# A hybrid decoder layer: early gathered rows issued behind the fortieth scatter column, and eight of the gathered tile instead of sixteen

## The chip, the core and the metric

The kernel runs on one core of one Trainium2 chip. Its engines work side by side, each through its own list of instructions: TensorE (PE in the profile; PEld are its weight loads), VectorE (DVE), ScalarE (ACT), GpSimd (POOL) and SyncE (SP, which here only issues DMAs). GpSimd issues the indirect DMAs, by which rows are gathered from DRAM or single numbers scattered into it. The metric is the device time of one execution in microseconds (us), as the median of several.

## The reference, cut to what matters

One layer for 528 positions of width 1024: two branches (a diagonal state space model and a matrix memory) are merged, and then comes the part that the change touches, a retrieval from 16384 experts. For each of the 512 output positions and each of 8 heads it scores 2 x 128 keys, takes the 16 best pairs, and adds up the chosen experts' output rows.

```python
def block(xb):
    q = (xb @ w_q).astype(f32).reshape(PEER_TOKEN_BLOCK, PEER_HEADS, 2, PEER_HALF)
    s = jnp.einsum('thid,hikd->thik', q, keys32)
    sv, si = lax.top_k(s, PEER_TOPK)
    ...
    cs, ci = lax.top_k(cand, PEER_TOPK)
    eidx = jnp.take_along_axis(cidx, ci, axis=-1)
    gate = jax.nn.softmax(cs, axis=-1)
    ug = u_tab[eidx]
    act = jax.nn.gelu(jnp.einsum('td,thkd->thk', xb, ug).astype(f32))
    vg = v_tab[eidx]
    return jnp.einsum('thk,thkd->td', (gate * act).astype(vg.dtype), vg)
```

Each chosen expert has a row of 1024 numbers in `u_tab` (dotted with the position's vector to give an activation) and one in `v_tab` (added to the output with the weight gate times activation).

## The kernel before, in words

The 512 positions are four tiles of 128. Tiles 1, 2 and 3 (but for the last 32 positions of tile 3) go the dense way. For every one of the 128 first keys j, `hidden` (line 1090) multiplies 128 experts' u rows with the 352 positions, all of them: 8 blocks of 3 matmuls, since each number is split into a high part `uh` (ACT, line 82) and a low part `ul` (DVE, line 83). Which experts were really chosen is then put in by gate tables. `gates` (line 1441) builds them for 32 positions at a time: DVE compares indices and weights them (tiles `o12` and `ow`, both tt at line 1049), PE multiplies the two into PSUM (tile `gp`, line 1496), ACT copies that to `stg`, and SP writes `stg` to DRAM. One block of 32 positions, of tile 1, comes otherwise: `scatter` (line 1412) has POOL add its gates into DRAM, one column of 128 numbers with one indirect DMA (tile `gds`, line 1416). There are 96 columns, 12 to a head, and the first column of a head waits until those of the head before it have landed.

Tile 0 and the last 32 positions of tile 3 go the sparse way: their rows are gathered. A gather is one indirect DMA on POOL that brings 128 rows of 1024 numbers (512 KB) into a tile; its use on DVE is one product with accumulation over those 1024 numbers. For the 32 positions of tile 3 there are 32 gathers of u rows (line 1360, index tile `xsi`, used at line 1368). For tile 0 there are 128 of u rows and 128 of v rows (line 1139, index tile `e0`, used at lines 1146 and 1154).

Three stages matter here.

- While the gate tables are built, the 32 gathers of tile 3 and the first NEARLY = 16 of tile 0 are done early (`ge0` to `ge47`). They have NE = 6 buffers: `ge6` takes the buffer of `ge0` and so on.
- In the main loop (line 1633), over the 128 second-stage keys j, PE multiplies the weighted gates with v rows (tile `o`, 18 matmuls an iteration) and, in 44 iterations, does a `hidden` that was not done before. The other 256 - NEARLY gathers of tile 0 (`g16` to `g255`) are spread evenly over it, with 7 buffers of their own.
- `gi` is the load of the gate tables for 8 values of j in the loop, from what `gates` and `scatter` wrote.

The order in the first stage is planned while the program is built. `clock` counts the time of PE's work so far (0.48 us for a block of `hidden`, 0.46 per pass for a gate group), `done` counts DVE's, and `fill` (line 1523) hands out `hidden` work so that PE's share keeps step with DVE's. `fill` calls `beside` (line 1380), which plans POOL's list with a time `t` of its own: a column advances it by 2.2 (5.0 at a head's first), a gather by 1.65 (3.0 if no columns are left), and it stops when it is ahead of `clock`. Each gather is due LAG = 24 after that time; when `clock` has reached this, its use is placed behind DVE's latest instructions (`pinned`, line 1373). POOL keeps the order of its list. At run time nothing waits for `clock`: an instruction runs when its data and its buffer are there and those ahead of it on its engine are done.

The lines of `beside` that decide between a gather and a column, before:

```python
if e["got"] < e["may"] and e["got"] - e["used"] < NE and (e["turn"] or not cols):
    n, e["turn"] = e["got"], 0
    ...
elif cols:
    scatter(1)
    e["turn"] = e["columns"] % 4
```

So after a column whose number is not a multiple of 4 a gather may follow. `may` is 0 until the indices `xsi` stand in the program, 32 from there, and 32 + NEARLY once `e0` does.

Of the kernel before, what the change touches and what calls it, by code (L numbers as in the profile page):

```python
# [66 lines left out]
def tile_hybrid_block(ctx: ExitStack, tc: tile.TileContext, a: dict, out: bass.AP, dbg: dict | None = None):  # L67
# [59 lines left out]

    xh, xl, blanks = front(tc, a, dbg, cst, dram, xnp, ident, h2d, xsd, gds, x0, qt01, dump, split, mm3, rsqrt, rsqrt_cols)
    peer(tc, a, out, dbg, cst, dram, xh, xl, blanks, ident, h2d, xsd, gds, x0, qt01, dump, split, mm3, rsqrt_cols)


# [894 lines left out]
def peer(tc, a, out, dbg, cst, dram, xh, xl, blanks, ident, h2d, xsd, gds, x0, qt01, dump, split, mm3, rsqrt_cols):  # L1026
# [10 lines left out]
    NREST = NKEY // 2 - LEFT // 2  # L1037
    SPP = [k + LEFT // 2 for k in range(NREST) if k * NSP // NREST != (k - 1) * NSP // NREST]
    SP_ = [2 * k + n for k in SPP for n in range(2)]
    NEARLY = 16  # L1040
    NSIDE = MS * P // P
    LAST = 3

# [8 lines left out]
    with es:  # L1052
# [129 lines left out]
        for n in (0, 1):  # L1182
            r = 0
            x = [sum(CNT[:r]) if n == 0 else CNT[r - 1] if r else 0 for r in range(TOPK)]
            while r < (8, TOPK)[n]:
                e = r + 1
# [144 lines left out]
        cols = []  # L1331


        NE = 6
        LAG = 24.0
        early = dict(t=8.0, columns=0, due=[], got=0, used=0, may=0, turn=0, last=None)

        def spread():

# [15 lines left out]
        def fetch_early(n, t):  # L1355

            if n >= NSIDE:
                return fetch(n - NSIDE, t)
            rows["s", n] = t
            return GP.indirect_dma_start(out=t, out_offset=None, in_=a["u"],  # L1360
                                         in_offset=bass.IndirectOffsetOnAxis(ap=xsi[:, n:n + 1], axis=0))

        def use_early(n):

            if n >= NSIDE:
                return pinned(use(n - NSIDE))
            g = rows.pop(("s", n))
            pinned(V.scalar_tensor_tensor(g, g, 1.0, xrep, op0=OP.mult, op1=OP.mult,
                                          accum_out=hsi[:, n:n + 1]))
            if n == NSIDE - 1:  # L1370
                sided()
# [8 lines left out]
        def beside(flush=False):  # L1380


            e = early
            while True:
                t = 1e9 if flush else clock[0]
                while e["due"] and e["due"][0] <= t:
                    e["due"].pop(0)
                    use_early(e["used"])
                    done[0] += 1.3
                    e["used"] += 1  # L1390
                if e["t"] > t:
                    break
                e["t"] = max(e["t"], clock[0] - 8.0)
                if e["got"] < e["may"] and e["got"] - e["used"] < NE and (e["turn"] or not cols):
                    n, e["turn"] = e["got"], 0
                    k = n % NE
                    if k < 4:
                        r = up.tile([P, D], F32, tag="vraw", name=f"ge{n}", bufs=4)
                    else:
                        r = rw.tile([P, D], F32, tag=f"early{k}", name=f"ge{n}", bufs=1)  # L1400
                    e["last"] = tc.keep_in_program_order(fetch_early(n, r))
                    e["t"] += 1.65 if cols else 3.0
                    e["due"].append(e["t"] + LAG)
                    e["got"] += 1
                elif cols:
                    scatter(1)
                    e["turn"] = e["columns"] % 4
                    e["t"] += 2.2 if e["columns"] % CH_ else 5.0
                elif e["got"] == e["may"] or not flush:
                    break  # L1410

        def scatter(n):

            early["columns"] += len(cols[:n])
            for ix, wt, c in cols[:n]:
                i_ = GP.indirect_dma_start(out=gds.rearrange("i g b j t -> (i g b j t)").unsqueeze(1),  # L1416
                                           out_offset=bass.IndirectOffsetOnAxis(ap=ix[:, c:c + 1], axis=0),
                                           in_=wt[:, c:c + 1], in_offset=None, compute_op=OP.add)

                h = c // CH_  # L1420
                if c % CH_ == 0:
                    heads.append([])
                for o in heads[h]:
                    tc.declare_no_dep(i_.ins, o.ins, reason="columns of one head")
                for o in heads[h - 1] if h else blanks:
                    behind(i_, o)
                heads[h].append(i_)
                behind(i_, lows[-1])
                if early["last"]:
                    tc.add_manual_dep(i_.ins, early["last"].ins.name, mybir.DependencyInfo(  # L1430
                        mybir.DependencyClass.NoSync, mybir.DependencyReason.DATA), reason="order")
            del cols[:n]
# [87 lines left out]

        whole = 4 * 24 + 40 * 2.5 + (NSIDE + NEARLY) * 1.3 + 3

        def fill(us):

            done[0] += us
            if paced[0]:
                beside()
            while todo and (ntodo - len(todo)) * whole < done[0] * ntodo:
                j, h = todo.pop(0)
                hidden(j, 2 * h, 2 * h + 2)  # L1530
# [26 lines left out]
        def more():  # L1557
            yield from filled(2)
            yield from filled(0)
            placed(prs[0][1].rearrange("p h k -> p (h k)"), 0)  # L1560
            V.tensor_copy(e0, prs[0][1].rearrange("p h k -> p (h k)"))
            early["may"] = NSIDE + NEARLY
        rest = more()
# [5 lines left out]
        assert early["used"] >= NSIDE, early  # L1569
        gates(3, rest, [P // TB - 1])  # L1570
        beside(True)
        for j, h in todo:
            hidden(j, 2 * h, 2 * h + 2)
# [14 lines left out]
        def products(i, j, wh, wl, vh, vl, pin=None, halves=(0, 1)):  # L1588
            s_ = slice(i * P, (i + 1) * P)
            for c in halves:  # L1590
                cc = slice(c * 512, (c + 1) * 512)
                last = mm3(op_[i][:, cc], wh[:, s_], wl[:, s_], vh[:, cc], vl[:, cc], j == 0, j == NKEY - 1, pin)
            return last
# [37 lines left out]
        due = 0  # L1631
        loop[0] = True
        for j in range(NKEY):
# [21 lines left out]

            upto = min(j + 1, NKEY - 6) * (2 * P - NEARLY) // (NKEY - 6)
            for last in (0, 1):
                while due < (upto if last else min(due + 1, upto)):
                    n = NEARLY + due
                    due += 1  # L1660
# [18 lines left out]
            if j < NKEY - LAST:  # L1679
                for i in range(NTD):  # L1680
                    last = products(i, *ops[j])
# [93 lines left out]
```

## Time and profile before

| | us |
|---|---|
| median of 3 runs | 1694.6 (1692.6 to 1696.47) |
| profiled execution, its own time | 1700.12 |
| its span, first to last instruction | 1698.2 |
| early rows: from the first early gather's issue (661.7) to the last early use (about 946) | 284.3 |
| main loop, from about 976 to about 1676 | 700 |

In rows of the profile, a name such as `ge<-ge,qt` says what an instruction writes and reads, `xN` how many instructions a row groups, and a bracket at the end of a row, as in `[3.53 <-DMA ge<-in_u,xsi]`, how long the engine was idle before it and what ended that. PEclk is TensorE's granted clock as a share of full speed. Matmuls follow each other before the one ahead is through, so PE's busy time is no measure of its work; its idle time is.

### The profile page before, as it was taken

What the parts mean: (1) busy time and instruction counts of PE and PEld (TensorE: products, weight loads), DVE (VectorE), ACT (ScalarE), POOL (GpSimd) and SP (SyncE); (2) the same over time, 40 slices, a digit from 0 to 9 for tenths busy, and PEclk for the clock granted to TensorE, in tenths of its full rate; (3) what the DMA queues carried; (4) which work ended last, traced back from release to release, by engine and by line L of the source; (5) the groups of instructions that cost most, each with busy time, mean ns of one, the idle gap of its engine ahead of it and who ended that gap; (6) DMA issues with size and microseconds to landing.
All of it is one profiled execution on the core that took longest, in us unless ns stands there. A gap on an engine that the chain in (4) does not pass through costs nothing. (4 is left out here: it accounts for less than half of the span.)

```text
span 1698.2 us, 25640 instructions
## 1 busy us (share of the span) xinstructions
PE 1631.2 (96%) x9551; PEld 1441.0 (85%) x9551; DVE 1318.4 (78%) x2639; ACT 710.3 (42%) x1159; POOL 685.7 (40%) x474
## 2 busy tenths in 40 slices
PE   7999999999999999979988899999999999999997
PEld 7898787878888899979988888888888888888885
DVE  6996733366579899979876497887979879797986
ACT  4544554433333254546544533333433334333334
POOL 2000032222132663677777243343434556554630
PEclk9999999999999999989989999999999999999998
DMA  4514252214453266889988999998989999999973
GB/s 177 126 51 112 96 186 92 63 38 135 165 186 116 31 189 207 264 269 322 308 283 300 355 367 379 349 392 312 402 314 400 369 367 376 398 351 357 376 266 123
DMA packets 147957, 423.20 MB, mean 249 GB/s; under 512 B 38228, under 2 KB 56788, under 8 KB 138360
## 3 DMA queue, kind: packets, MB, share of 16 engines
q1 hardware_dynamic: 86184, 263.00, 43.6%
q0 software_dynamic: 55360, 151.07, 25.5%
q10 hardware_dynamic: 6288, 7.49, 1.4%
q8 instruction: 75, 1.23, 0.3%
q14 instruction: 50, 0.41, 0.1%
HBM read 376.13 MB, written 45.38 MB: 248 GB/s over the span
## 5 line engine op out<-in xcount | busy, mean ns | idle before, releaser
L90 PE MATMUL h<-x2h,ul 128*128 128x352 f32 x1024 | 335.7, 328 | 13.4 <-DVE ul L83 13.4
L86 PE MATMUL h<-x2h,uh 128*128 128x352 f32 x1024 | 335.3, 327 | 0.3 <-ACT act L1102 0.2
L89 PE MATMUL h<-x2l,uh 128*128 128x352 f32 x1024 | 334.3, 326 | 0.0
L86 PE MATMUL o<-vh,wh 128*128 128x512 f32 x768 | 283.9, 395 | 11.8 <-ACT wh L1651 11.7
L89 PE MATMUL o<-vl,wh 128*128 128x512 f32 x768 | 283.1, 394 | 0.8 <-DVE vl L83 0.8
L90 PE MATMUL o<-vh,wl 128*128 128x512 f32 x768 | 270.3, 391 | 0.0
L1139 POOL DMA_INDIRECT g<-in_v,e x128 | 196.0, 1531 | 161.8 <-DVE ac L1154 151.7
L82 ACT ACTIVATE vh<-v 128x1024 fp32r<-128x1024 f32 x128 | 135.1, 1058 | 192.8 <-PE o L90 178.3
L1416 POOL DMA_INDIRECT gds<-cw,ix x96 | 183.4, 1910 | 73.1 <-issue 46.6
L1139 POOL DMA_INDIRECT g<-in_u,e x112 | 125.4, 1120 | 212.6 <-DVE g L1146 204.0
L90 PEld LDWEIGHTS h<-x2h,ul 128*128 128x128 f32 x1024 | 195.0, 190 | 16.4 <-DVE ul L83 15.0
L82 ACT ACTIVATE uh<-u 128x1024 fp32r<-128x1024 f32 x128 | 134.4, 1059 | 172.2 <-PE h L89 159.2
L86 PEld LDWEIGHTS h<-x2h,uh 128*128 128x128 f32 x1024 | 195.9, 191 | 3.9 <-ACT act L1102 0.8
L89 PEld LDWEIGHTS h<-x2l,uh 128*128 128x128 f32 x1024 | 195.7, 191 | 1.9
L86 PEld LDWEIGHTS o<-vh,wh 128*128 128x128 f32 x768 | 144.9, 190 | 41.0 <-ACT wh L1651 13.2
L83 DVE TENSOR_TENSOR vl<-v,vh 128x1024 fp32r<-128x1024 f32 x128 | 155.9, 1218 | 25.1 <-ACT vh L82 25.1
L89 PEld LDWEIGHTS o<-vl,wh 128*128 128x128 f32 x768 | 146.3, 191 | 31.1 <-DVE vl L83 1.1
L90 PEld LDWEIGHTS o<-vh,wl 128*128 128x128 f32 x768 | 145.1, 189 | 31.0 <-DVE wl L1666 0.3
L83 DVE TENSOR_TENSOR ul<-u,uh 128x1024 fp32r<-128x1024 f32 x128 | 155.0, 1216 | 16.5 <-ACT uh L82 16.5
L1154 DVE SCALAR_TENSOR_TENSOR ac<-g,w,ac 128x1024 f32<-128x1024 f32 x127 | 162.2, 1277 | 0.0
L1146 DVE SCALAR_TENSOR_TENSOR g<-g,x 128x1024 f32<-128x1024 f32 x112 | 136.4, 1218 | 0.0
L1651 ACT ACTIVATE wh<-w 128x384 fp32r<-128x384 f32 x128 | 66.5, 520 | 107.7 <-DVE w L1646 101.9
(553 smaller groups left out, 3038.8 us busy)
## 6 DMA issues: line engine op xcount, KB each, us to landing
u<-in_ut SPq DMA_DIRECT2D x64, 1024.0 KB, 7.0
v<-in_v SPq DMA_DIRECT2D x128, 512.0 KB, 7.6
gd<-stg SPq DMA_DIRECT2D x9, 2048.0 KB, 9.2
gi<-gd SPq DMA_DIRECT2D x16, 1152.0 KB, 14.2
ad<-act SPq DMA_DIRECT2D x38, 352.0 KB, 4.7
act<-ad SPq DMA_DIRECT2D x38, 352.0 KB, 9.8
wq<-in_w_q SPq DMA_DIRECT2D x14, 512.0 KB, 3.6
gds<-qt SPq DMA_DIRECT2D x6, 1024.0 KB, 5.2
```

What stands on the lines that cost most here:

```text
L82: A.activation(hi, src, AF.Copy)
L83: return eng.tensor_tensor(lo, src, f32(hi), op=OP.subtract)
L86: i_ = PE.matmul(ps, lh, rh, start=first, stop=False)
L89: PE.matmul(ps, lh, rl, start=False, stop=False)
L90: return PE.matmul(ps, ll, rh, start=False, stop=last)
L1139: return GP.indirect_dma_start(out=t, out_offset=None, in_=a["u"] if s_ < P else a["v"], in_offset=bass.IndirectOffsetOnAxis(ap=e0[:, c:c ...
L1146: i_ = V.scalar_tensor_tensor(g, g, 1.0, x0, op0=OP.mult, op1=OP.mult, accum_out=hsl[:, c:c + 1])
L1154: i_ = V.scalar_tensor_tensor(ac0, g, w0[:, c:c + 1], ac0, op0=OP.mult, op1=OP.add)
L1416: i_ = GP.indirect_dma_start(out=gds.rearrange("i g b j t -> (i g b j t)").unsqueeze(1), out_offset=bass.IndirectOffsetOnAxis(ap=ix[:, c:c ...
L1651: A.activation(wh, w, AF.Copy)
```

## The change

Only the plan changes; no arithmetic does. NEARLY goes from 16 to 8: eight gathers of tile 0 with their uses move out of the early stage to the loop, which then has 248 instead of 240. The rule of turns goes. A gather may now stand in POOL's list only once 40 columns (C0) have been placed, and only when `t` has reached `next`, which moves on by PACE = 4.7 with each gather but may lag behind `t` by up to two paces. Where no columns are left, gathers keep to `next` too. LAG is 28 instead of 24.

```diff
-    NEARLY = 16
+    NEARLY = 8
...
-        LAG = 24.0
-        early = dict(t=8.0, columns=0, due=[], got=0, used=0, may=0, turn=0, last=None)
+        LAG = 28.0
+        PACE = 4.7
+        C0 = 40
+        early = dict(t=8.0, columns=0, due=[], got=0, used=0, may=0, next=0.0, last=None)
...
-                if e["got"] < e["may"] and e["got"] - e["used"] < NE and (e["turn"] or not cols):
-                    n, e["turn"] = e["got"], 0
+                if not cols:
+                    e["t"] = max(e["t"], e["next"])
+                    if e["t"] > t:
+                        break
+                if e["got"] < e["may"] and e["got"] - e["used"] < NE and e["columns"] >= C0 and e["t"] >= e["next"]:
+                    n, e["next"] = e["got"], max(e["next"], e["t"] - 2 * PACE) + PACE
...
-                    e["t"] += 1.65 if cols else 3.0
+                    e["t"] += 1.65
                     e["due"].append(e["t"] + LAG)
                     e["got"] += 1
                 elif cols:
                     scatter(1)
-                    e["turn"] = e["columns"] % 4
                     e["t"] += 2.2 if e["columns"] % CH_ else 5.0
```

What this does to POOL's list where the early rows begin, just behind the last low part that POOL computes for the queries. `gds` rows are columns, `ge` rows gathers with their number, and `xN` counts equal rows. Before:

```order
L1416 DMA gds_67<-cw1_4880,ix1_4879 1572864x1 x23
L1360 DMA ge0_6198<-in_u,xsi_4326 128x1024
L1416 DMA gds_67<-cw1_4880,ix1_4879 1572864x1 x2
L1360 DMA ge1_6264<-in_u,xsi_4326 128x1024
L1416 DMA gds_67<-cw1_4880,ix1_4879 1572864x1
L1360 DMA ge2_6336<-in_u,xsi_4326 128x1024
```

With the change, the same place (the column's line is now 1421, the gather's 1362):

```order
L1421 DMA gds_67<-cw1_4880,ix1_4879 1572864x1 x36
L1362 DMA ge0_6593<-in_u,xsi_4326 128x1024
L1362 DMA ge1_6621<-in_u,xsi_4326 128x1024
L1362 DMA ge2_6623<-in_u,xsi_4326 128x1024
L1362 DMA ge3_6651<-in_u,xsi_4326 128x1024
L1421 DMA gds_67<-cw1_4880,ix1_4879 1572864x1 x2
L1362 DMA ge4_6729<-in_u,xsi_4326 128x1024
L1421 DMA gds_67<-cw1_4880,ix1_4879 1572864x1
L1362 DMA ge5_6783<-in_u,xsi_4326 128x1024
L1421 DMA gds_67<-cw1_4880,ix1_4879 1572864x1 x5
L1362 DMA ge6_6966<-in_u,xsi_4326 128x1024
L1362 DMA ge7_7015<-in_u,xsi_4326 128x1024
```

With 4 columns ahead of what is shown, 27 columns stood before `ge0` and 40 do now; 69 and 56 are left behind it. Gathers stood one at a time between columns; now `ge0` to `ge3` stand together, and `ge6` to `ge9` do.

The uses of these rows in DVE's list, in the same stretch of gate groups (`ow` and `o12` are gate tiles, `ul` low parts for `hidden`, the second number after `ge` is a buffer's). Before:

```order
L1049 TENSOR_TENSOR ow312_6877<-o12312_6876,wb30_6168 128x2048
L1368 SCALAR_TENSOR_TENSOR ge6_6582,hsi_4327<-ge6_6582,qt01_69 128x1024
L1368 SCALAR_TENSOR_TENSOR ge7_6653,hsi_4327<-ge7_6653,qt01_69 128x1024
L1368 SCALAR_TENSOR_TENSOR ge8_6712,hsi_4327<-ge8_6712,qt01_69 128x1024
L83 TENSOR_TENSOR ul67_7265<-u33_7222,uh67_7264 128x1024
L1049 TENSOR_TENSOR ow313_7035<-o12313_7034,wb30_6168 128x2048
L1368 SCALAR_TENSOR_TENSOR ge9_6760,hsi_4327<-ge9_6760,qt01_69 128x1024
```

With the change:

```order
L83 TENSOR_TENSOR ul66_7241<-u33_7238,uh66_7240 128x1024
L1049 TENSOR_TENSOR ow313_6942<-o12313_6941,wb30_6189 128x2048
L1370 SCALAR_TENSOR_TENSOR ge0_6593,hsi_4327<-ge0_6593,qt01_69 128x1024
L1370 SCALAR_TENSOR_TENSOR ge1_6621,hsi_4327<-ge1_6621,qt01_69 128x1024
L1370 SCALAR_TENSOR_TENSOR ge2_6623,hsi_4327<-ge2_6623,qt01_69 128x1024
L1370 SCALAR_TENSOR_TENSOR ge3_6651,hsi_4327<-ge3_6651,qt01_69 128x1024
L1370 SCALAR_TENSOR_TENSOR ge4_6729,hsi_4327<-ge4_6729,qt01_69 128x1024
L1198 MATCH_REPLACE tkc007_7411<-cs0_6897,cand00_6899 128x50
L83 TENSOR_TENSOR ul67_7286<-u33_7238,uh67_7285 128x1024
```

At the gate group 313, where row 9 was used, now row 0 is; five uses stand in one run.

The end of POOL's early list and the beginning of the loop's gathers (`g` rows), with the change:

```order
L1421 DMA gds_67<-cw1_4880,ix1_4879 1572864x1 x4
L1139 DMA ge36_8784<-in_u,e0_4323 128x1024
L1421 DMA gds_67<-cw1_4880,ix1_4879 1572864x1
L1139 DMA ge37_8860<-in_u,e0_4323 128x1024
L1139 DMA ge38_8862<-in_u,e0_4323 128x1024
L1139 DMA ge39_8864<-in_u,e0_4323 128x1024
L1421 DMA gds_67<-cw1_4880,ix1_4879 1572864x1 x7
L1139 DMA g8_9726<-in_u,e0_4323 128x1024
```

Before, `ge47` was the last early row, and the loop's gathers began with `g16`.

## The prediction, made before the changed kernel ran

> **What bounds the kernel now.** I began with the page's busy shares, cut the span into stages, asked in each who waited for whom, and then followed single waits in the timeline. The first line is the page's; the others are windows: start and end, length, busy time (instructions) of PE, PEld, DVE, ACT, POOL, then granted clock, DMA share, GB/s.
>
> ```profile
> PE 1631.2 (96%) x9551; PEld 1441.0 (85%) x9551; DVE 1318.4 (78%) x2639; ACT 710.3 (42%) x1159; POOL 685.7 (40%) x474
> 600.00:661.70 61.70, 61.70 (x410) 61.05 (x409) 60.00 (x276) 27.95 (x37) 26.73 (x15) 1.00 0.61 184
> 661.70:946.00 284.30, 259.78 (x1926) 253.07 (x1925) 234.08 (x370) 152.07 (x188) 206.55 (x118) 0.95 0.89 290
> 976.00:1676.00 700.00, 691.13 (x3312) 597.47 (x3311) 596.86 (x783) 263.31 (x469) 313.58 (x233) 0.99 0.94 355
> ```
>
> PE is the bound over the whole, but not in every stage. Just before the early rows it never idles; in the loop it idles 9 of 700 us. In the stage of the early rows (661.7 to 946) it idles 24.5 of 284.3, and its clock is down. Who waited there (engine, line, what for: total, times, longest):
>
> ```profile
> PE h L90 <- DVE ul L83: 12.2, 5, 5.3
> PE gp L1496 <- DVE ow L1049: 12.1, 2, 6.7
> DVE ge L1368 <- DMA ge<-in_u,xsi: 18.1, 6, 7.1
> DVE ge L1146 <- DMA ge<-in_u,e: 16.6, 3, 8.8
> POOL gds L1416 <- issue: 35.9, 63, 10.8
> POOL gds L1416 <- DMA gds<-cw,ix: 20.8, 6, 11.4
> POOL ge L1360 <- DVE xsi L1344: 26.7, 1, 26.7
> ```
>
> PE waited 24.3 us for DVE, and DVE 34.7 us for gathered rows. That one causes the other shows in the timeline (start, length, engine; a bracket is the idle time before). Row 12 goes out at 735.88 and lands at 748.28; DVE, whose list is fixed, stands in front of its use, and behind that use stands the gate tile `ow` for which PE idles 5.40. Row 40 did the same at 902.79 with a low part `ul`.
>
> ```profile
> 735.88 1.40 POOL L1360 DMA_INDIRECT ge<-in_u,xsi  x1 [0.30 <-issue]
> 748.28 1.23 DVE L1368 SCALAR_TENSOR_TENSOR ge<-ge,qt 128x1024 f32<-128x1024 f32 x1 [7.14 <-DMA ge<-in_u,xsi]
> 749.56 1.20 DVE L1049 TENSOR_TENSOR ow<-o,wb 128x2048 f16<-128x2048 f16 x1
> 750.82 1.87 PE L1496 MATMUL gp<-ow,o 128*128 128x128 f16 x16 [5.40 <-DVE ow L1049]
> 902.79 1.22 DVE L1146 SCALAR_TENSOR_TENSOR ge<-ge,x 128x1024 f32<-128x1024 f32 x1 [7.53 <-DMA ge<-in_u,e]
> 905.21 0.66 PE L90 MATMUL h<-x2h,ul 128*128 128x352 f32 x1 [5.33 <-DVE ul L83]
> ```
>
> After four such waits the clock stood at half. Windows over these periods:
>
> ```profile
> 726.70:730.10 3.40, 3.40 (x13) 3.40 (x13) 3.36 (x6) 0.00 (x0) 2.79 (x3) 0.51 0.72 263
> 750.70:757.40 6.70, 5.02 (x27) 4.75 (x27) 6.70 (x12) 3.75 (x4) 4.09 (x3) 0.50 0.55 161
> 870.10:880.30 10.20, 5.60 (x29) 5.61 (x30) 8.03 (x11) 2.08 (x3) 8.68 (x6) 0.50 0.70 198
> 904.30:911.00 6.70, 5.79 (x20) 5.79 (x21) 6.70 (x7) 0.00 (x0) 3.49 (x3) 0.50 0.63 189
> ```
>
> PE was busy 3.40 + 5.02 + 5.60 + 5.79 = 19.8 us in them, at half speed, so 9.9 us were lost. PE's own work in the stage is 284.3 - 24.3 - 9.9 = 250.1 us.
>
> Why are rows late? POOL's groups in this stage (count, busy, mean ns):
>
> ```profile
> L1416 POOL DMA_INDIRECT gds<-cw,ix x69 | 136.1, 1972 | 56.6 <-issue 35.9 <-DMA gds<-cw,ix 20.8
> L1360 POOL DMA_INDIRECT ge<-in_u,xsi x32 | 49.3, 1541 | 37.7 <-DVE xsi L1344 26.7 <-issue 7.6 <-DVE ge L1368 1.9
> L1139 POOL DMA_INDIRECT ge<-in_u,e x16 | 20.1, 1255 | 4.9 <-issue 4.6 <-DVE wb L1467 0.3
> 711.33 2.50 POOL L1416 DMA_INDIRECT gds<-cw,ix  x1 [10.83 <-issue]
> ```
>
> With the 0.30 us between two issues a column costs 2.27, a row of tile 3 1.84, one of tile 0 1.56: 69 x 2.27 + 32 x 1.84 + 16 x 1.56 = 240.5. To this come the long waits at a head's first column: 56.7 - 69 x 0.30 = 36 for five heads, 7.2 each (the last line is one). Together 276.5 us, more than PE's 250.1: **in this stage POOL's list is the bound**, and it reaches PE through rows that land after DVE wants them. Before `ge0`, POOL stood 26.7 us idle for the indices `xsi`, with columns waiting behind.
>
> **The change, part by part.**
>
> Columns first. The thirteen columns that now stand ahead of `ge0` cost 13 x 2.27 = 29.5 us and one head's wait, and run in those 26.7 idle us. Sixty-nine columns behind `ge0` become 56, and eight rows leave: 56 x 2.27 + 32 x 1.84 + 8 x 1.56 = 198.5, and with four heads at 7.2, 227 us (with 11.4, the longest, 244). Both are below 250.1, so PE's own work becomes the longest.
>
> Rows later, LAG 28. POOL cannot use all of that, since `ge6` needs the buffer of `ge0`. From the use of row 0 to that of row 39 the changed order holds 936 `hidden` and 440 gate matmuls; by the starts of the rows below (0.16 apart, and 16 gate matmuls in 1.10, thus 0.058) PE needs 149.8 + 25.5 = 175 us. In that time POOL has rows 6 to 39 and 41 columns: 26 x 1.84 + 8 x 1.56 + 41 x 2.27 + 28.8 = 182. It falls about 7 us behind by the end, where it fell 276.5 - 250 = 26 behind before. A planned 28 minus 7 leaves 21 for landings, which took 12.4 for row 12.
>
> ```profile
> 866.58 0.32 PE L89 MATMUL h<-x2l,uh 128*128 128x352 f32 x1
> 866.74 0.32 PE L90 MATMUL h<-x2h,ul 128*128 128x352 f32 x1
> 898.79 1.10 PE L1496 MATMUL gp<-ow,o 128*128 128x128 f16 x16
> ```
>
> What each saves: all waits gone, 24.3 + 9.9 = 34.2; none gone, 0. Since rows 0 to 3 and 6 to 9 go out together and share a buffer round, I keep one late round, at the price of the shortest wait that halved the clock: 3.33 us idle, and half of 3.40. **-34.2 + 5.0 = -29.2.**
>
> ```profile
> 726.51 0.49 PE L90 MATMUL h<-x2h,ul 128*128 128x352 f32 x1 [3.33 <-DVE ul L83]
> ```
>
> Runs of uses. Five uses now stand one behind another. Six did before, from 834.18, and PE idled 1.64 behind them, after waits for rows as well. With 234.1 - 8 x 1.3 = 224 us of work beside PE's 250, DVE recovers; I take nothing, at most 1.6 for each of two runs of five.
>
> ```profile
> 834.18 1.22 DVE L1368 SCALAR_TENSOR_TENSOR ge<-ge,qt 128x1024 f32<-128x1024 f32 x1
> 839.17 1.22 DVE L1368 SCALAR_TENSOR_TENSOR ge<-ge,qt 128x1024 f32<-128x1024 f32 x1 [0.32 <-DMA ge<-in_u,xsi]
> 847.40 0.43 PE L90 MATMUL h<-x2h,ul 128*128 128x352 f32 x1 [1.64 <-DVE ul L83]
> ```
>
> Eight rows in the loop. DVE gets 8 x (1.22 + 0.08) = 10.4 us more; it is busy 597 of the loop's 700, so this lies beside PE. POOL is busy 314. The DMA gets 8 x 512 KB = 4.2 MB: at 355 GB/s 11.8 us, with a share of 0.94 now. Without cover that is the upper bound. PE's waits in the loop:
>
> ```profile
> PE o L86 <- ACT wh L1651: 11.7, 5, 3.7
> DVE w L1646 <- DMA gi<-gds: 26.0, 5, 7.1
> 1068.63 0.96 PE L86 MATMUL o<-vh,wh 128*128 128x512 f32 x3 [2.03 <-ACT wh L1651]
> 1159.74 1.25 PE L86 MATMUL o<-vh,wh 128*128 128x512 f32 x3 [2.03 <-ACT wh L1651]
> 1068.70:1072.00 3.30, 3.30 (x15) 2.74 (x16) 3.30 (x6) 0.63 (x2) 0.98 (x1) 1.00 0.69 270
> 1159.80:1163.20 3.40, 3.40 (x9) 2.71 (x10) 3.40 (x6) 0.63 (x2) 0.98 (x1) 0.56 0.00 0
> ```
>
> No wait of DVE for a loop row stands there; the waits come with the gate load `gi`, five in 240 rows. Eight rows more make that 0.2 of a wait of some 3 us: **+0.5**. Below, if these waits went, -11.7; I see no reason, the loads and their order stay.
>
> **Sum:** -29.2 + 0.5 = -28.7, from the profiled execution's 1700.1 to 1671.4. It is 5.5 us above the median of the three runs; against that, 1694.6 - 28.7 = **1665.9, thus 1666 us**. If the 5.5 lie in these very waits, 1671.
>
> **The rivals.** They differ in how many of the seven buffer rounds (40 rows, 6 buffers) still land late.
>
> *Half a cure (0.20).* For it: the rows do not come one at a time at even distances, the order shows groups of three and four, and POOL's 182 against 175 leaves it behind again at the end. Two rounds late, each like row 34's wait (8.84 us on DVE, 6.70 on PE, half of 5.60): 2 x 9.5 = 19 back, 1694.6 - 34.2 + 19 = 1679. Short waits may cost more than themselves: the two equal idles of 2.03 above were followed by a clock of 1.00 and of 0.56, so 2.0 or 3.7 each. The Trainium skill, "TensorE: Matmul & The Clock Gate", section "Why this matters for your kernels", has only idle gaps over about 3 us drop the clock; by it three leftovers of 2 us would give back 6 us, by the dearer row 11. The second of the two rows speaks against it.
>
> ```profile
> 872.27 1.23 DVE L1146 SCALAR_TENSOR_TENSOR ge<-ge,x 128x1024 f32<-128x1024 f32 x1 [8.84 <-DMA ge<-in_u,e]
> 874.70 1.57 PE L1496 MATMUL gp<-ow,o 128*128 128x128 f16 x13 [6.70 <-DVE ow L1049]
> ```
>
> *The loop pays (0.10).* If the DMA has no room, the 11.8 us come in full: -29.2 + 11.8, 1677. Against it: DVE waits for no loop row.
>
> *No change (0.09).* Three or four late rounds, 28.5 to 38, eat the 34.2.
>
> *Slower (0.08).* One mechanism: a group's rows, issued back to back, land one after another while their uses stand in a run, so that every round is late once. At 9.5 a round the balance turns at 3.6 rounds; five cost 47.5, 1708, all seven 66.5, 1727. The Trainium skill, "DMA: Bandwidth & Descriptors", section "SWDGE vs HWDGE vs iDMA", has one queue for all that GpSimd issues, which would put such rows in line; no row here separates the two. Against it: eight rows less, and 28 instead of 24 to land in.
>
> **How the numbers follow.** The forecast has 0.53. Faster by over 0.2% (what a measurement here can tell from no change, 3.4 us): 0.53 + 0.20 + 0.10 = 0.83; same 0.09; slower 0.08. The range begins at 1656, everything gone (1660.4) and a third of the loop's 11.7, and ends at 1690, above 1679 with the loop's 11.3. It leaves out no change, slower, and a little below.
>
> **What would show it.** In the changed profile: POOL's idle before `xsi` gone and filled with columns; DVE's waits for `ge` rows from 34.7 down to under 10; PE's waits for `ul` and `ow` in this stage from 24.3 to about 3, with at most one period of half clock; the stage at about 255 us for 284; the loop at 700 as before. It is wrong if DVE still waits over 15 us for rows, if PE waits for `ul` without a late row ahead (then runs of uses are the cause), or if the loop grows by more than 3 us.

## The result, and the profile after

| | before | after |
|---|---|---|
| median of 4 runs each, us | 1693.6 (1691.54 to 1696.47) | 1669.62 (1667.19 to 1670.33) |
| profiled execution, its own time | 1700.12 | 1670.1 |
| its span | 1698.2 | 1668.4 |
| first `o` matmul of the main loop | 975.7 | 950.2 |

The ratio of the runs is 0.9855 (95% interval 0.9836 to 0.9873). Between the medians lie 24.0 us, between the two profiled executions 30.0. Of these 30.0, 25.5 are there when the loop begins. The forecast was 1666 us, in a range of 1656 to 1690. Two executions in the experiments below took several times as long as the others of their kernel (4850 and 9161 us); the ratios leave them out.

The page of the changed kernel first (busy time, share of the span and instructions of each engine), then its windows, with the columns of the prediction's: start and end, length, PE, PEld, DVE, ACT, POOL, granted clock, DMA share, GB/s. The second window ends 30 us before the loop, as the prediction's did.

```profile
PE 1620.0 (97%) x9551; PEld 1429.4 (86%) x9551; DVE 1318.1 (79%) x2639; ACT 708.3 (42%) x1159; POOL 709.4 (43%) x474
```

```profile
600.00:661.70 61.70, 61.21 (x400) 60.56 (x399) 59.76 (x275) 28.38 (x38) 48.76 (x26) 1.00 0.64 174
661.70:920.00 258.30, 250.27 (x1915) 243.50 (x1915) 228.30 (x378) 147.12 (x183) 194.72 (x101) 0.99 0.89 304
743.50:750.30 6.80, 3.66 (x12) 3.21 (x12) 6.80 (x11) 2.43 (x3) 5.88 (x4) 0.50 0.46 83
950.00:1646.00 696.00, 686.68 (x3315) 593.21 (x3314) 605.61 (x799) 265.63 (x473) 330.28 (x241) 1.00 0.96 364
```

The stage took 258.3 us where it had taken 284.3. PE idles 258.3 - 250.27 = 8.0 us in it, after 24.5 before. One stretch of half clock is left (third line; two periods of 3.4 us), in which PE was busy 3.66 us, so 1.8 are lost, after 9.9. PE's own work is then 258.3 - 8.0 - 1.8 = 248.5 us, beside 250.1 before: that part has stayed. In the first line POOL is busy 48.76 of the 61.7 us ahead of the stage, where it had been busy 26.73: the columns have gone there.

Who waits in the stage, from 661.7 to 920 (engine, line, what for: total, times, longest):

```profile
PE h L90 <- DVE ul L83: 5.3, 4, 3.1
PE h L86 <- ACT uh L82: 1.4, 1, 1.4
PE h L86 <- ACT act L1102: 1.2, 2, 0.8
DVE ul L83 <- ACT uh L82: 10.9, 7, 3.3
DVE ge L1370 <- DMA ge<-in_u,xsi: 9.7, 4, 4.8
POOL ge L1362 <- DVE ge L1370: 19.1, 6, 17.5
```

PE's wait for `ow` is gone and that for `ul` went from 12.2 to 5.3. DVE waits 9.7 us for rows instead of 34.7. In the last line POOL now waits for DVE, 19.1 us where it had waited 1.9. Row 6 stood ready for 17.53 us because row 0, whose buffer it takes, hadn't been used. A list that waits for its consumer is no longer behind it.

The rest is seen in the timeline (start, length, engine; the bracket is the idle time before).

```profile
668.79 1.01 POOL L1362 DMA_INDIRECT ge<-in_u,xsi  x1 [1.17 <-DVE ei L1458]
719.27 1.74 POOL L1362 DMA_INDIRECT ge<-in_u,xsi  x1 [17.53 <-DVE ge L1370]
737.94 1.22 DVE L1370 SCALAR_TENSOR_TENSOR ge<-ge,qt 128x1024 f32<-128x1024 f32 x1
741.37 1.22 DVE L1370 SCALAR_TENSOR_TENSOR ge<-ge,qt 128x1024 f32<-128x1024 f32 x1
742.52 1.22 DVE L1049 TENSOR_TENSOR m<-ge,rkd 128x2048 f16<-128x2048 f16 x1
746.00 2.35 DVE L83 TENSOR_TENSOR ul<-u,uh 128x1024 fp32r<-128x1024 f32 x2
747.26 0.66 PE L90 MATMUL h<-x2h,ul 128*128 128x352 f32 x1 [3.14 <-DVE ul L83]
757.61 15.42 POOL L1362 DMA_INDIRECT ge<-in_u,xsi  x1 [0.30 <-DVE wb L1472]
779.76 1.23 DVE L1370 SCALAR_TENSOR_TENSOR ge<-ge,qt 128x1024 f32<-128x1024 f32 x1 [3.55 <-DMA ge<-in_u,xsi]
811.46 1.23 DVE L1370 SCALAR_TENSOR_TENSOR ge<-ge,qt 128x1024 f32<-128x1024 f32 x1 [4.76 <-DMA ge<-in_u,xsi]
815.77 0.42 PE L90 MATMUL h<-x2h,ul 128*128 128x352 f32 x1 [1.70 <-DVE ul L83]
```

POOL stands 1.17 us idle before `ge0`, where it stood 26.7. PE's longest wait, 3.14 us, has **no late row ahead of it**: from 737.94 DVE does four uses (rows 6 to 9, the first and the last are shown), then work for the pairs, all without a gap, and only then the `ul` that PE is waiting for. The stretch of half clock lies here. It began at 743.5, a little before PE stopped at 744.12, behind waits of 1.45 and 0.49 us for ACT; PE was busy 0.63 us in its first period and 3.04 in its second. The wait of 1.70 at 815.77 stands behind a late row, the one at 811.46.

### The profile page after: what moved, and what is told of

Read it like the earlier page. It is cut to its first block, busy times and chain, and to the rows that moved or that the text cites. A ratio compares the mean times of both kernels' runs of the same rounds, so it can differ in the third digit from the quotient of the medians.

```text
span 1668.4 us, 25647 instructions
## 1 busy us (share of the span) xinstructions
PE 1620.0 (97%) x9551; PEld 1429.4 (86%) x9551; DVE 1318.1 (79%) x2639; ACT 708.3 (42%) x1159; POOL 709.4 (43%) x474
## 3 DMA queue, kind: packets, MB, share of 16 engines
q0 software_dynamic: 55360, 151.07, 25.5%
## 4 chain that ended last, share of the span: by engine, by line
PE 80%; DVE 8%; DMA 5%; ACT 2%; issue 2%; POOL 2%; ACTq 0%; DVEq 0%; POOLq 0%
PE o L86 10%; PE o L90 10%; PE o L89 10%; PE h L86 8%; PE h L90 8%; PE h L89 8%; PE q L89 1%; PE gp L1501 1%; PE q L90 1%; PE q L86 1%; DMA wo<-in_w_out 1%; PE s L877 1%; PE n L886 1%; POOL ge L1362 1%; DMA ge<-in_u,xsi 1%
## 5 line engine op out<-in xcount | busy, mean ns | idle before, releaser
L86 PE MATMUL o<-vh,wh 128*128 128x512 f32 x768 | 279.6, 391 | 7.7 <-ACT wh L1656 7.5
L89 PE MATMUL o<-vl,wh 128*128 128x512 f32 x768 | 278.9, 390 | 0.8 <-DVE vl L83 0.8
L90 PE MATMUL o<-vh,wl 128*128 128x512 f32 x768 | 266.3, 390 | 0.9 <-DVE wl L1671 0.9
L1139 POOL DMA_INDIRECT g<-in_v,e x128 | 202.2, 1580 | 146.5 <-DVE ac L1154 129.5
L1139 POOL DMA_INDIRECT g<-in_u,e x120 | 135.2, 1126 | 214.1 <-DVE g L1146 195.4
L1146 DVE SCALAR_TENSOR_TENSOR g<-g,x 128x1024 f32<-128x1024 f32 x120 | 145.9, 1217 | 0.0
```

Of the source, the lines that this page charges most:

```text
L86: i_ = PE.matmul(ps, lh, rh, start=first, stop=False)
L89: PE.matmul(ps, lh, rl, start=False, stop=False)
L90: return PE.matmul(ps, ll, rh, start=False, stop=last)
L1146: i_ = V.scalar_tensor_tensor(g, g, 1.0, x0, op0=OP.mult, op1=OP.mult, accum_out=hsl[:, c:c + 1])
```

## The experiments

My theory after this result: POOL's list was behind because its columns stood behind the wait for `xsi`; the forty columns ahead of it cure that, and what is left comes from uses that stand in runs. The rivals: the later due time alone does it; the eight rows less do it; the even distances do it; or the uses were the fault all along. Each kernel changes a few numbers or a line. The table puts them together: median and ratio to the kernel before with the 95% interval, then of each one's profiled execution DVE's waits for `ge` rows, PE's waits for `ul` and `ow` (640 to 946), and the start of the loop. The waits are sums of the views' lines; where the view puts a wait at a use down to "issue" (10.4 us with C0 = 0, 1.0 or less elsewhere), it is counted in. The medians of before in the three series of experiments were 1695.8 to 1697.1; each ratio is to its own series.

| kernel | median us | ratio | DVE for rows | PE for ul, ow | loop starts |
|---|---|---|---|---|---|
| before, first series | 1693.6 | 1 | 34.7 | 24.3 | 975.7 |
| the change | 1669.62 | 0.9855 (0.9836-0.9873) | 9.7 | 5.3 | 950.2 |
| the change, again | 1668.25 | 0.9831 (0.9803-0.9858) | 2.6 | 3.7 | 947.1 |
| before, LAG 28 | 1693.6 | 0.9992 (0.9963-1.002) | 32.5 | 19.2 | 973.4 |
| before, eight rows | 1690.36 | 0.9945 (0.9924-0.9965) | 23.9 | 14.5 | 968.1 |
| before, forty columns | 1682.23 | 0.9911 (0.988-0.9943) | 18.9 | 8.5 | 952.9 |
| before, one use a visit | 1691.86 | 0.9972 (0.9951-0.9993) | 30.9 | 29.2 | 977.8 |
| change, sixteen rows | 1668.39 | 0.9821 (0.9777-0.9865) | 8.6 | 6.4 | 952.4 |
| change, LAG 24 | 1678.34 | 0.9892 (0.9845-0.9939) | 8.8 | 5.4 | 959.5 |
| change, C0 = 0 | 1695.74 | 0.9989 (0.9969-1.0009) | 24.2 | 20.9 | 975.1 |
| change, no early rows | 1663.2 | 0.9797 (0.9757-0.9837) | none | not known | not known |
| change, one use a visit | 1662.13 | 0.979 (0.975-0.9829) | 0.0 | 2.2 | 943.8 |

### One part alone, on the kernel before

Eight rows of tile 0 early, not sixteen:

```diff
-    NEARLY = 16
+    NEARLY = 8
```

> The kernel before with eight early rows of tile 0 instead of sixteen, and nothing else. My theory (POOL's list is longer than PE's work in the stage, so rows land late): the list is shorter by 8 rows and 2 columns, 17 us of 276.5, still some 10 us longer than PE's 250; rows get late less often, about half of the gain: DVE's waits for early rows 10 to 20 us (34.7 before), ratio 0.990 to 0.995. Rival 'due time' (rows are late because the plan uses them 24 after the issue, and 28 mends it): no gain, ratio 0.998 to 1.002, waits for rows as before but for the eight that left.

The later due time:

```diff
-        LAG = 24.0
+        LAG = 28.0
```

> The kernel before with LAG 28 instead of 24, and nothing else. My theory: POOL's list is as long as before, so it runs behind as before, and 4 us more for each row mends a part at most: ratio 0.994 to 1.000, DVE's waits for rows over 20 us. Rival 'due time': most of the gain, ratio 0.986 to 0.990, waits for rows under 12 us.

The condition of forty columns, with the old turns:

```diff
-                if e["got"] < e["may"] and e["got"] - e["used"] < NE and (e["turn"] or not cols):
+                if e["got"] < e["may"] and e["got"] - e["used"] < NE and e["columns"] >= 40 and (e["turn"] or not cols):
```

> The kernel before with one condition more: no early row before 40 columns are placed (16 rows of tile 0, LAG 24, turns as before). My theory: 14 columns move into POOL's idle time ahead of the indices, the list behind it is 55 columns and 48 rows, 209 us and about 29 of waits, below PE's 250: most of the gain, ratio 0.985 to 0.990, DVE's waits for rows under 12 us. Rival 'due time' and rival 'eight rows' (what saves is the smaller amount of early work): no gain, ratio 0.998 to 1.002.

LAG alone is nothing that can be measured (0.9992). DVE still waits 32.5 us for rows, so a later due time by itself doesn't help a list that goes on falling behind. Eight rows less give about a third of the gain, with 23.9 us of row waits, a little more than I had expected. The forty columns give 0.9911, short of the 0.985 to 0.990 that I had expected, with more row waits too. Its runs spread from 1671.93 to 1686.31, and the profiled execution is the fastest of them, so its waits are probably at the low end. Most of them are for the rows of tile 0, the last in POOL's list (tile 0 in the first line, tile 3 in the second):

```profile
DVE ge L1146 <- DMA ge<-in_u,e: 14.6, 5, 5.3
DVE ge L1368 <- DMA ge<-in_u,xsi: 4.1, 3, 1.7
```

In the kernel before these two stood at 16.6 and 18.1: forty columns ahead heal most of the waits for tile 3 and leave those for tile 0 nearly as they were. Alone they bring 14.8 us, where the whole change brings 24.0 to 27.5.

### One part taken back, in the changed kernel

Sixteen rows again:

```diff
-    NEARLY = 8
+    NEARLY = 16
```

> The changed kernel with sixteen early rows of tile 0 again. My theory: the columns moved ahead are enough, ratio 0.984 to 0.990 as with the change (0.9855), the last rows of the stage a little later. Rival 'eight rows': most of the gain is lost, ratio over 0.993.

LAG back at 24:

```diff
-        LAG = 28.0
+        LAG = 24.0
```

> The changed kernel with LAG 24 again. My theory (the length of POOL's list sets how late rows land): the list is the same and its lateness at the end the same, so 4 us less for each row costs a few waits: DVE's waits for early rows 10 to 20 us (9.7 with the change), ratio to before 0.983 to 0.990. Rival (the later use is a needed half of the change): ratio over 0.992, waits for rows over 25 us.

Rows as soon as `xsi` is there, the rest of the change kept:

```diff
-        C0 = 40
+        C0 = 0
```

> The changed kernel without the rule of the fortieth column: rows may begin as soon as their indices are there, still at most one in 4.7 us of planned time, with LAG 28 and eight rows of tile 0. 28 columns stand ahead of row 0. My theory: the list behind row 0 is 68 columns and 40 rows, 226 us and 36 of waits, 261 against PE's 250: half a gain, ratio 0.988 to 0.994, DVE's waits for rows 15 to 25 us. Rival (even distances and the later use do it): as with the change, 0.982 to 0.987.

**Sixteen rows** are as fast as eight (0.9821, with an interval that holds both measurements of the change): beside the columns the eight rows bring nothing that can be measured. The ratio is a little below the forecast. **Without the forty columns** all of the gain is gone, more than I had expected, even what eight rows bring alone (0.9945); even distances and a later use don't hold by themselves. The timeline of that kernel shows POOL, DVE and PE, and the last line is POOL's group of columns from 661.7 to 946:

```profile
668.01 1.01 POOL L1362 DMA_INDIRECT ge<-in_u,xsi  x1 [34.96 <-DVE ei L1458]
847.08 1.22 DVE L1370 SCALAR_TENSOR_TENSOR ge<-ge,qt 128x1024 f32<-128x1024 f32 x1 [11.00 <-DMA ge<-in_u,xsi]
849.51 0.66 PE L90 MATMUL h<-x2h,ul 128*128 128x352 f32 x1 [6.87 <-DVE ul L83]
L1421 POOL DMA_INDIRECT gds<-cw,ix x68 | 143.2, 2106 | 37.1 <-issue 31.2 <-DMA gds<-cw,ix 6.0
```

POOL stands idle 34.96 us before `ge0`, 68 columns are left behind it (56 in the changed kernel), and a row comes 11.00 us late for which PE waits 6.87. That is much like the kernel before, and the change does nothing without the columns ahead of the wait for `xsi`. Not all of the 34.96 us is the columns' doing: `xsi` itself is written at 667.57 here and at 661.26 in the kernel before. So it is in the other profiles of the table, at 665.8 to 668.4 with eight rows and at 661.2 to 663.0 with sixteen; why stays open. (The bracket names `ei`, DVE's instruction right behind `xsi`.)

**LAG 24** costs 8.7 us beside the change's first median; the runs of the two don't overlap, the intervals of the ratios just do. Row waits were 8.8, under the 10 to 20 that I had expected and between the 9.7 and 2.6 of the change's two profiles. What PE lost stands in its timeline:

```profile
742.90 0.66 PE L86 MATMUL h<-x2h,uh 128*128 128x352 f32 x1 [4.70 <-ACT act L1102]
814.63 0.43 PE L90 MATMUL h<-x2h,ul 128*128 128x352 f32 x1 [4.95 <-DVE ul L83]
```

and DVE's ahead of the second:

```profile
808.62 1.23 DVE L1370 SCALAR_TENSOR_TENSOR ge<-ge,qt 128x1024 f32<-128x1024 f32 x1 [4.96 <-DMA ge<-in_u,xsi]
810.84 1.23 DVE L1370 SCALAR_TENSOR_TENSOR ge<-ge,qt 128x1024 f32<-128x1024 f32 x1 [0.99 <-issue]
812.20 1.23 DVE L1370 SCALAR_TENSOR_TENSOR ge<-ge,qt 128x1024 f32<-128x1024 f32 x1
813.35 2.36 DVE L83 TENSOR_TENSOR ul<-u,uh 128x1024 fp32r<-128x1024 f32 x2
```

One late row, 4.96 us, became 4.95 of PE, because two more uses stood between it and the `ul`, the first of them after an idle of 0.99. In the changed kernel, with one use between, a wait of 4.76 became 1.70. Ahead of the other long wait, for ACT, ACT was busy without a gap from 733.71, with two table loads of 1.28 us each among its work; in the changed kernel the same two loads stood some 4 us earlier. What moved them I did not trace.

### The floor, and runs of uses

The forty early gathers left out:

```diff
-                    e["last"] = tc.keep_in_program_order(fetch_early(n, r))
+                    rows[("s", n) if n < NSIDE else n - NSIDE] = r
...
-            pinned(V.scalar_tensor_tensor(g, g, 1.0, xrep, op0=OP.mult, op1=OP.mult,
+            pinned(V.scalar_tensor_tensor(g, xrep, 1.0, xrep, op0=OP.mult, op1=OP.mult,
...
-                i_ = V.scalar_tensor_tensor(g, g, 1.0, x0, op0=OP.mult, op1=OP.mult, accum_out=hsl[:, c:c + 1])
+                i_ = V.scalar_tensor_tensor(g, x0 if c < NEARLY else g, 1.0, x0, op0=OP.mult, op1=OP.mult, accum_out=hsl[:, c:c + 1])
```

> The changed kernel without its 40 early gathers: their uses on DVE stay where they are but multiply tiles that are there already (the early rows' products are left out of the result). No row can be late. My theory: DVE's waits for rows 0; what PE still idles in the stage comes from runs of DVE work: the 3.1 us wait behind the run of four uses (747 in the changed kernel) stays, the 1.9 us wait behind row 19 goes; the loop begins at 942 to 948 (950.2 with the change), ratio 0.978 to 0.984. Rival (every stall of PE here is a late row): PE does not wait for low parts at all, the loop begins before 942.

At most one use placed at a visit of `beside`:

```diff
             e = early
+            left = 1000 if flush else 1
             while True:
                 t = 1e9 if flush else clock[0]
-                while e["due"] and e["due"][0] <= t:
+                while left and e["due"] and e["due"][0] <= t:
+                    left -= 1
```

> The changed kernel with at most one use placed at a time, so that uses stand singly on DVE from row 17 on and in runs of two or three before. My theory: the run of four uses that holds PE up is gone, with its half clock: 3 to 6 us less in the stage, but the last uses stand later and four of them in a run near its end; ratio 0.980 to 0.986. Rival (runs of uses cost nothing): no difference to the change, 0.984 to 0.987.

Without any late row the changed kernel takes 1663.2 us. Its waits, and with them half of what I had expected, are not known. With all rows gathered and the uses spread it takes 1662.13 (1661.55 to 1662.23), the same. **This version beats both kernels**, the change by 6.1 to 7.5 us by the medians; the runs of the two don't overlap. It came out a little below the forecast. DVE has no wait for a row left; PE's waits in its stage are these:

```profile
PE h L90 <- DVE ul L83: 2.2, 1, 2.2
PE h L86 <- ACT act L1102: 0.2, 1, 0.2
```

So spreading ended the run's own stall and the row waits as well. It also makes uses a little later, so both may have a part in it. Whether eight rows matter once uses are spread stays open: with sixteen this plan does not come out, its list ends with 37 of the 48 early rows placed.

### Were runs of uses the fault all along?

The same edit on the kernel before:

> The kernel before with one edit: at most one use of an early row is placed at a visit of the planner, so that uses move apart; columns, turns, sixteen rows and LAG 24 stay. My theory (POOL's list falls behind, and the columns ahead of the first row are what cures that; runs of uses are only what is left afterwards): rows still land late, DVE waits 15 to 35 us for rows, ratio 0.985 to 1.0. Rival (runs of uses were the fault all along, and the fortieth column only happened to move them): waits for rows under 10 us and a ratio of 0.983 or less, no worse than the whole change.

and the change once more beside it:

> The changed kernel as it is, again, so that the two kernels of this call stand beside it on one chip. Expected: 0.9855 of the kernel before, as in its first measurement, within 0.002.

The edit on the kernel before gives 0.9972 and leaves the waits (DVE for rows of tile 3 and tile 0, PE for `ow` and `ul`):

```profile
DVE ge L1368 <- DMA ge<-in_u,xsi: 17.0, 5, 6.9
DVE ge L1146 <- DMA ge<-in_u,e: 13.9, 3, 7.0
PE gp L1498 <- DVE ow L1049: 19.3, 5, 7.9
PE h L90 <- DVE ul L83: 9.9, 3, 4.2
```

The rival falls: while POOL is behind, spreading uses cures almost nothing; once it isn't, it is worth 6.1 to 7.5 us. The change itself came out at 0.9831, a little below what I had expected and with overlapping intervals. Its second profile has the same stall behind the same run of uses, and the rest of the waits are smaller:

```profile
744.86 0.66 PE L90 MATMUL h<-x2h,ul 128*128 128x352 f32 x1 [3.35 <-DVE ul L83]
```

## Why the prediction was right, step by step

**POOL's list is the bound, and the columns lift it: right.** POOL's idle before `ge0` went from 26.7 to 1.17, columns fill the time ahead, and POOL waits for DVE's buffers instead of DVE for POOL. That the columns are what the rest needs is shown by C0 = 0 (nothing left of the gain) and by sixteen rows (all of it left). They are not the whole: alone they bring 0.9911. LAG 28, which alone brings nothing, is worth some 9 us beside them and the rest of the change. The even distances were not tested apart; with LAG 24 the change (0.9892) can't be told from the columns alone, so distances and fewer rows show no gain of their own there.

**The sum of POOL's list: near, with one price off.** POOL's groups of the changed kernel, 661.7 to 920 (count, busy, mean ns):

```profile
L1421 POOL DMA_INDIRECT gds<-cw,ix x59 | 115.3, 1954 | 25.3 <-issue 16.8 <-DMA gds<-cw,ix 6.7 <-DMA ge<-in_u,xsi 1.8
L1362 POOL DMA_INDIRECT ge<-in_u,xsi x32 | 65.3, 2040 | 28.3 <-DVE ge L1370 19.1 <-issue 6.5 <-DVE ei L1458 1.2
L1139 POOL DMA_INDIRECT ge<-in_u,e x8 | 12.2, 1529 | 2.4 <-issue 1.8 <-DVE o L1049 0.3 <-DVE wb L1472 0.3
```

Three of the 59 columns stand ahead of `ge0`. A column costs 1.95 + 0.30 = 2.25 us, as reckoned (2.27). A row of tile 3 took 2.04 us for the 1.54 of before, mostly because of a single one that took 15.42 (below): without it, (65.3 - 15.42) / 31 = 1.61. The waits at a head's first column came to 25.3 - 59 x 0.30 = 7.6 where I had put four of 7.2. So the two misses of 16 and 21 us went against each other, and that the total came out near is luck in that part.

**-29.2 in the stage: a little too much.** The stage became 26.0 us shorter. Idle time gave 24.5 - 8.0 = 16.5 of it and the clock 9.9 - 1.8 = 8.1; the windows' ends, which are not the same work, leave 1.4.

**Runs of uses at nothing: the term that was mis-sized.** I wrote that DVE recovers and priced a run at no more than 1.6. The share of busy time hid that the uses stand ahead of one particular `ul`: four of them (1.15 us from start to start) followed by the pair work cost PE 3.14 us, and 1.5 of the 1.8 us of half clock lie behind that wait (half of 3.04). I had kept 5.0 for one late round. The leftover was 8.0 + 1.8 = 9.8: nearly half of it, 3.14 + 1.5, came with the run, and the stall behind a late row was only 1.70. The condition that I had given, PE waiting for `ul` without a late row ahead, came true at this one place. Spreading the uses gives 6.1 to 7.5 us, about what this mistake and the last row waits are worth. One result doesn't fit this account: without early gathers the uses stand in the same run, so its stall should stay, and still that kernel is 5.0 to 6.4 us faster than the change. It also takes 40 issues off POOL and their bytes off the DMA; which of this helps is open.

**LAG 28: right in direction, for another reason.** I argued with landings. With 24 DVE's waits for rows (8.8 us) lay between those of the change's two profiles, yet PE's long stalls grew; one of the two long ones is a late row with a run of uses between itself and the `ul`. The other, behind ACT, was not explained.

**The loop at +0.5: the profiled pair says -4, and nothing puts that down to the change.** The loop's window took 696 us for 700. Four periods of half clock, 3.4 us each, stood in the profiled loop of before (its window has a granted clock of 0.99) and none in this one. In the kernel with LAG 28 alone, whose loop also has 240 gathers, the same window has the full clock (1.00):

```profile
976.00:1676.00 700.00, 693.32 (x3350) 599.85 (x3348) 594.36 (x785) 268.64 (x477) 309.12 (x230) 1.00 0.93 350
```

So such periods need not come with 240 gathers, and half of 4 x 3.4, that is 6.8 us, would cover the 5.5 by which the execution of before lay above its median. But they don't set that execution apart: its granted clock over the whole span is 0.984, and the experiments' executions of before that took 1693 to 1698 us have 0.982 to 0.986. Why the pair shows -30.0 and the medians -24.0 and -27.5 (1695.77 to 1668.25) stays open. From the loop's start to the span's end the change took 718.2 and 718.4 us. The other profiles have 716.5 to 720.8 with eight rows and 713.7 to 722.5 with sixteen, so what eight rows more cost the loop can't be told from them. PE's waits for `wh` and DVE's for the gate load in the changed kernel's loop:

```profile
PE o L86 <- ACT wh L1656: 7.5, 6, 1.7
DVE w L1651 <- DMA gi<-gds: 0.9, 2, 0.5
```

The 26.0 us that DVE waited for `gi` are gone, for which I had seen no reason. They are no part of the gain: with C0 = 0, which is as slow as before, that line reads 0.9 as well.

**The rivals.** "The loop pays" and "slower by late groups" fell. Rows do go out four together, and they were not late as a group. "Half a cure" was right in that leftovers cost more than I kept, but they are 9.8 us, not the 19 of two late rounds.

## What to carry to other kernels

On an engine that keeps the order of its list, work that waits for nothing belongs ahead of the first entry that waits: here moving eight entries out of a full stage counted for less than filling the idle time before it. When an engine with spare time gets short jobs in a row, price the run by the first result behind it that the bound engine is waiting for, not by the spare time. And before a profiled execution is used as the base of a sum, compare the stages that the change leaves alone with other profiles: here the time from the loop's start to the end differed by 8.8 us among them, with no relation to the rows.

## What was not expected of the hardware

One gather issue took 15.42 us on POOL where the others of its group take 0.98 to 4.09. It was the fourth of four in a row. In the second profile of the change the same four took at most 1.95 each, and the column right behind them took 10.41:

```profile
755.18 10.41 POOL L1421 DMA_INDIRECT gds<-cw,ix  x1 [0.30 <-issue]
```

The other groups of four in these kernels show no such thing, and with LAG 24 a column took 8.44 us behind no such group, so four in a row is not the cause by itself. In all three cases DVE worked meanwhile on gate tiles, low parts and pair work, and POOL came free 0.6 to 1.5 us after the first use of a row on DVE (772.39 in the changed kernel, 783.63 with LAG 24) or the first gap there (764.11 in the second profile). No run varies this, so what holds POOL stays open.

A short idle of PE can be enough for the half clock. In the version with one use a visit, PE idled 2.21 us before 752.05, and the clock was at half around it:

```profile
751.80:755.20 3.40, 3.15 (x11) 3.16 (x12) 3.40 (x6) 0.44 (x1) 3.01 (x2) 0.50 1.01 386
```

In the changed kernel the waits of 1.45 and 0.49 for ACT lie in the 3.4 us ahead of the drop at 743.5 (first two lines). The wait of 1.70 at 815.77 was followed by none (last line):

```profile
740.10:743.50 3.40, 1.47 (x14) 1.04 (x11) 3.40 (x7) 3.40 (x6) 2.79 (x3) 1.00 1.04 331
743.50:746.90 3.40, 0.63 (x2) 0.17 (x1) 3.40 (x5) 2.43 (x3) 3.09 (x2) 0.50 0.55 116
815.80:819.20 3.40, 3.40 (x21) 3.40 (x22) 3.40 (x4) 1.49 (x3) 2.79 (x3) 1.00 0.90 221
```

With LAG 24 three waits of 0.69, 0.35 and 0.46 us, one soon after the other, were followed by a granted clock of 0.51 from 876.3 to 879.7. So the idle time need not be in one piece.

The Trainium skill, "TensorE: Matmul & The Clock Gate", section "Why this matters for your kernels", asks for no idle gaps over about 3 us; here a wait of 2.21 went with a drop, so the bound that these runs show is lower.
